# Turned input fetched piece by piece over the second down sweep, and a fourth raw buffer that lies in its last quarter

## The chip, the cores and the metric

One core of one Trainium2 chip. The metric is the device time in microseconds (us) of one launch, the median of three runs. The engines are named as the profile names them: PE (TensorE) for matmuls, PEld its weight loads, DVE (VectorE), ACT (ScalarE), POOL (GpSimd), SP (SyncE, which here only issues DMAs). A "q" behind a name (SPq, POOLq, ACTq) is that engine's instruction queue where it issues DMAs.

## The reference

Two layers over 256 tokens of width D = 2048 in float32. Layer 0 mixes tokens by a convolution module, layer 1 by latent attention; each is followed by the same kind of MLP, and a final RMSNorm ends the kernel. The change touches the MLP only:

```python
def sq_relu_mlp(h, w1, w2):                 # w1 (2048, 8192), w2 (8192, 2048)
    return jnp.square(jax.nn.relu(h @ w1)) @ w2
...
    for layer in range(DEPTH):
        ...
        h = rms_norm(x, norm_mlp_g[layer])
        x = x + sq_relu_mlp(h, mlp_w1[layer], mlp_w2[layer])
    return rms_norm(x, final_norm_g)
```

## The kernel before

**Products in three terms.** Every float32 operand is split into an upper part `hi` (ACT copies it to a narrower format, L460) and a lower part `lo` (DVE subtracts, L461), and a product is three matmuls, `mm3` (L213 to L215): hi by hi, lo by hi, hi by lo. Weights are split as they arrive; a "raw" buffer of 1 MB takes the load from HBM, and rings of `hi` and `lo` tiles (`WB` = 6) take its halves.

**The turned input.** The MLP's input is held transposed, in both parts: 16 blocks k of 128 features, each 2 KB in a partition, 32 KB in all (`xt`). It lies at the right end of the on-chip memory in two pools, one inside the other: level 0 holds blocks 0 to 3, level 1 holds blocks 4 to 7 in one tile and 8 to 15 in another. `open_xt` and `open_rest` open them, `xrows` finds a block.

**Two halves, and in each an up stage and two down sweeps.** `mlp` goes over the 8192 hidden features in two halves. A half first runs the up stage: 8 groups of 4 units, each unit one load of 4 blocks of `w1` (unit u of a group needs blocks 4u to 4u + 3 of the turned input) and 32 matmuls (L806, L807). Then come two down sweeps, one for each half of the output columns, of 16 units each: 7 plain ones (`PlainQuad`, 24 matmuls) and 9 mixed ones (`MixedQuad`, 21 matmuls on sums of weight blocks and of inputs, a scheme with seven products for eight). The order in the second sweep, numbered 0 to 15 here, is P M M P M P M M P M P M M P M P. The first units of the next half's up stage are called 16, 17, ... below. This structure stands twice, once in each layer; in each layer only the first half is followed by another half.

**Queues written out by hand.** `run` goes through the units. At each it first issues the loads for which a buffer is free, on SP. Then it queues the splits: the second half of the unit itself, the first half of the next unit, then (for a mixed unit) the sums of weight blocks on DVE (L511, L515, L516) and the splits of those sums; then the unit's matmuls, and then what is in `u.after`. The entries of `free` are the free buffers; those in `held` are not used again. Engines run their own queues in order, and a queue stands while its first instruction waits.

**A fourth raw buffer in the down sweeps.** Three raw buffers (`raw`) serve all stages. During the sweeps the level 1 pool of the turned input is closed, and `open_down` (called after the last up unit) opens another in its place: `forms` (8 KB, the last group's split inputs, which the plain units 0 and 3 of the second sweep are the last to read), `rawd`, a fourth raw buffer (8 KB), four `rooms` (8 KB, from which POOL adds the first sweep's sums to `xs` by DMA, L600) and a small pad.

**Saving and fetching.** In the first half the blocks 4 to 15 are saved to HBM during the up stage (`save`, L882, 6 DMAs of 512 KB). In the second sweep `retire_raw` takes `rawd` out of use after unit 7, and after unit 11 the level 1 pool is opened again and the blocks are fetched (`fetch`, L885) on SP: 4 and 6 after unit 11, 8 and 10 after unit 12, 12 and 14 after unit 13. In the profile these are `xt<-spare`. In the second half nothing is saved; at its end the pools are opened again for layer 1's mixer, or `load_gf` puts the final gain `gf` at level 0 (L2089, L2090), which DVE multiplies in (L2094) towards the end.

Beside the weights, the up stage of each half loads the corners that the mixed units need: `copy_sum` (SP, L874) and `add_sum` (POOL, L877), HBM to HBM.

Of the kernel before, what the change touches and what calls it, by code (L numbers as in the profile page):

```python
# [11 lines left out]
F32 = mybir.dt.float32  # L12
F32R = mybir.dt.float32r
# [6 lines left out]
P = 128  # L20
D = 2048
KC = D // P
T = 2
S = T * P
FF = 4 * D
NB = 512
# [54 lines left out]
def trunk_kernel(  # L81
# [60 lines left out]
    def nm(s):  # L142
        uid[0] += 1
        return f"{s}_{uid[0]}"
# [171 lines left out]
    at, cols = 0, []  # L316
# [8 lines left out]
    xt_cx, xt = [ExitStack(), ExitStack()], []  # L325
# [27 lines left out]
    def right_pool(name, bufs, level=0):  # L353

        for i in (1, 0)[: 2 - level]:
            xt_cx[i].close()
            xt_cx[i] = ExitStack()
        return xt_cx[level].enter_context(tc.tile_pool(name=name, bufs=bufs, side="right", reuse_waits="tile"))

    ctx.callback(lambda: [xt_cx[i].close() for i in (1, 0)])  # L360

    def xt_tile(pool, n):
        return pool.tile([P, n, 2 * S], F32R, name=nm("xt"))

    def open_xt(name):
        xt[:] = [xt_tile(right_pool(name, 1), KC // 4)]
        open_rest(name + "r")

    def open_rest(name):
        pool = right_pool(name, 1, 1)  # L370
        xt[1:] = [xt_tile(pool, n) for n in (KC // 4, KC // 2)]

    def xrows(k, n):
        i = min(k // 4, 2)
        return xt[i][:, k - 4 * i : k - 4 * i + n, :]

    xhl = lambda k: xrows(k, 1)[:, 0, :]
    xh = lambda k: xhl(k)[:, :S]
    xl = lambda k: xhl(k)[:, S:]
    open_xt("xt0")  # L380
    scratch = main.tile([P, NB], F32, name="scratch")

# [306 lines left out]
    def mlp(layer, ssq, next_gain, finish=None, before=None, between=None, beside=None, after_up=None):  # L689

        with ExitStack() as cx:
# [19 lines left out]
            units, rstd = [], []  # L711
# [6 lines left out]
            def open_down(hf):  # L718
                pool = right_pool(f"dn{layer}{hf}", 1, 1)
                down["forms"] = [pool.tile([P, 4, S], F32R, name=nm(f"d{c}")) for c in "hl"]  # L720
                raw = pool.tile([P, 4 * NB], F32, name=nm("rawd"))
                down["rooms"] = [pool.tile([P, NB], F32, name=nm("room")) for _ in range(4)]
                pool.tile([P, PAD_DOWN], F32, name=nm("pad"))
                down["raw"] = lambda: raw
                free.append(down["raw"])
# [134 lines left out]
            def half(hf):  # L860

                last = hf == HALVES - 1
# [18 lines left out]
                def save(k):  # L881
                    nc.sync.dma_start(spare[:, k : k + 2, :], xrows(k, 2).bitcast(F32))  # L882

                def fetch(k):
                    nc.sync.dma_start(xrows(k, 2).bitcast(F32), spare[:, k : k + 2, :])  # L885
# [6 lines left out]
                for g in range(ng):  # L892
# [13 lines left out]
                    for u in range(KC // 4):  # L906
                        n = KC // 4 * g + u

                        def multiply(q, g=g, u=u, ps=ps):
                            if u == 0:  # L910
                                ps[:] = [psum_bank(4 * (g % 2) + b) for b in range(4)]
                            up_products(ps, u, q.parts)

                        after = [lambda k=k: copy_sum(k) for k in due_at.get(n, [])]
                        after += [lambda k=k: add_sum(k) for k in due_at.get(n - 1, [])]
                        if not last and u == 2 and 1 <= g <= 6:
                            after.append(lambda g=g: save(2 * g + 2))
                        if u == KC // 4 - 1:
                            after.append(lambda g=g, ps=ps: at_ticks(evacuation(g, gs, ps)))
                            if beside is not None and hf == 0 and g == 1:  # L920
                                tables = beside()
                                after.append(lambda: at_ticks([(11 + 2 * i, lambda: next(tables, None)) for i in range(7)]))
                        if n == n_slots - 1:
                            after.insert(0, lambda: open_down(hf))
                        unit(Step, rows(mlp_w1[layer], 4 * u, 4, c0, NB), multiply, (), after)
# [5 lines left out]
                def mixed_unit(sums, i):  # L931
                    g, b = ms[i]

                    def src():
                        top, low = row_of((sums.n, i))
                        return top[:, :NB], low, made[sums.n, i]

                    unit(MixedQuad, src, lambda q: sums.mixed(q, *gs[g][b], i == len(ms) - 1))

                def plain_unit(sums, k, at=(), end=False):  # L940
                    unit(
                        PlainQuad, rows(w, k_lo + k, 2, sums.n * NB, 2 * NB),
                        lambda q: sums.plain(q.parts, hi, lo, k, end), at,
                    )

                for n in range(0, NNB, 2):
                    sums = Sums(n, (0, 1) if n == 0 else () if last else (1,))
                    final = last and n == NNB - 2
                    order = ks if n == 0 else ks[-2:] + ks[:-2]
                    head = HEAD[n // 2]  # L950
                    tail = LAST_TAIL if final and finish is not None else 2 if final else 1
                    inner = len(order) - head - tail
                    m, start = 0, len(units)
                    for i, k in enumerate(order[: len(order) - tail]):
                        plain_unit(sums, k)
                        if i < head - 1:
                            continue
                        upto = -(-len(ms) * (i - head + 2) // (inner + 1))
                        while m < upto:
                            mixed_unit(sums, m)  # L960
                            m += 1
                    if final:
                        for i in range(2):
                            units[-4 + i].after.append(lambda i=i: prepare(i, what="s"))
                        break
                    plain_unit(sums, order[-1], [lambda sums=sums: sums.join(room)], True)
                    closing.append([lambda sums=sums, n=n: sums.close(down_room if n == 0 else room)])
                    if n:
                        units[start + 7].after.append(retire_raw)
                        units[start + 11].after.append(lambda: open_rest(f"xt{layer}{hf}"))  # L970
                        for i, k in enumerate(range(KC // 4, KC, 2)):
                            units[start + 11 + i // 2].after.append(lambda k=k: fetch(k))
                if not last:
                    return

# [12 lines left out]
                def middle():  # L988
                    for n in range(2):
                        prepare(n, what="t")  # L990

                open_rest(f"xt{layer}{hf}")
                for k in tail:
                    end = k == tail[-1]
# [9 lines left out]
            for hf in range(HALVES):  # L1004
                nssq = half(hf)
# [4 lines left out]
    with ExitStack() as cx:  # L1010
# [235 lines left out]
        with tc.manual_schedule():  # L1246
# [100 lines left out]
            upper_x, lower_x, last = ((0, 0),), ((0, 1),), ((1, 0),)  # L1347
# [48 lines left out]
            for c in range(1, KC + 1):  # L1396
                n = UC * c
# [121 lines left out]
            for m in range(NP):  # L1519
# [4 lines left out]
                for j in range(2):  # L1524
                    k = 2 * m + j
# [19 lines left out]
                for q in {NP - 3: (0, 1, 4), NP - 2: (5, 2, 3), NP - 1: (6, 7)}.get(m, ()):  # L1545
                    t, i = divmod(q, NNB)
# [80 lines left out]
    with ExitStack() as cx:  # L1627
        at = cx.enter_context(tc.tile_pool(name="at", bufs=1, reuse_waits="tile"))
# [22 lines left out]
        units, pieces = [], {}  # L1651
# [297 lines left out]
        with tc.manual_schedule():  # L1949
# [89 lines left out]
            for g in range(NG):  # L2039
                for i in range(HG):  # L2040
                    h = g * HG + i

                    n = -(-len(work) // (HG - i))
# [29 lines left out]
            prefetch()  # L2073

        open_xt("xt1")
        ssq, add, prepare = residual_stage(
            True, g_mlp[1], raw=cq.rearrange("p t n -> p (t n)").rearrange("p (k s) -> p k s", s=S), by_steps=(2, 3)
# [103 lines left out]
```

## Time and profile before

| | us |
|---|---|
| median of 3 runs | 1945.93 |
| lowest, highest | 1945.91, 1948.66 |
| profiled execution | 1943.44 |
| its span | 1941.7 |
| PE busy in the span | 1922.1 |
| DVE busy | 1541.8 |
| ACT busy | 1150.3 |
| POOL busy | 315.0 |

The profile is of one execution, and its times are from the span's start. Its lines give, in a timeline: start, duration, engine, line of the kernel, operation, what it writes and reads, shapes, how many such were merged, and in brackets the idle time before it with what ended it. In a list of waits: engine, tile and line, who was waited for, total us, times, longest. In a table of windows: the stretch, its length, busy time and count of PE, PEld, DVE, ACT and POOL, the granted TensorE clock as a share of full speed, the mean busy share of the 16 DMA engines, and GB/s.

### The profile page before, as it was taken

Reading aid. Unit: us, or ns where it says so; the run is one execution under the profiler, and the core shown is the slowest. Engines: PE = TensorE matmul, PEld = TensorE weight load, DVE = VectorE, ACT = ScalarE, POOL = GpSimd, SP = SyncE. Lnnn points to the kernel's source line nnn. Section 1 sums busy time; section 2 is a strip of 40 time slices with the busy share of each in tenths; the row PEclk is TensorE's granted clock in tenths of the full one; section 3 lists DMA queues with packets and bytes.
Section 4 is the critical chain, followed back from the end, with each engine's and each line's share of the span. In section 5 each row is a group of like instructions: output and inputs, shape, how many; then the busy total and the mean of one; then the engine's idle time right before and its main releaser. Section 6 shows DMA issues by size and latency. Waiting matters only on the chain.

```text
span 1941.7 us, 29140 instructions
## 1 busy us (share of the span) xinstructions
PE 1922.1 (99%) x10775; PEld 1678.7 (86%) x10775; DVE 1541.8 (79%) x2472; ACT 1150.3 (59%) x1736; POOL 315.0 (16%) x284
## 2 busy tenths in 40 slices
PE   8999999999999999999999999999999999999998
PEld 8999888888888888888899998888888878888886
DVE  7999987767988676698976665866689976668998
ACT  5667755565665555666676665555556655555665
POOL 6999200110010100001001310001000101000010
PEclk9999999999999999999999999999999999999999
DMA  7766456997687988668665445499866889886683
GB/s 230 212 188 183 158 189 208 280 287 233 225 242 232 289 257 250 191 222 234 211 193 155 130 143 184 163 267 290 261 203 212 241 283 277 245 252 222 197 257 131
DMA packets 252590, 428.50 MB, mean 221 GB/s; under 512 B 21144, under 2 KB 96160, under 8 KB 252192
## 3 DMA queue, kind: packets, MB, share of 16 engines
q1 hardware_dynamic: 234992, 394.75, 62.1%
q0 software_dynamic: 16128, 29.37, 9.3%
q10 hardware_dynamic: 1328, 2.52, 0.4%
q8 instruction: 84, 1.38, 0.3%
q14 instruction: 58, 0.48, 0.1%
HBM read 407.72 MB, written 46.14 MB: 234 GB/s over the span
## 4 chain that ended last, share of the span: by engine, by line
PE 92%; DVE 3%; issue 2%; ACT 1%; DMA 0%; POOL 0%; ACTq 0%; DVEq 0%; POOLq 0%
PE acc L806 24%; PE acc L213 14%; PE acc L215 14%; PE acc L214 14%; PE acc L807 13%; PE acc L1075 8%; PE acc L1538 2%; DVE sum L1162 1%; ACT hi L180 0%; DMA xs<-in_x 0%; PE acc L1928 0%; DVE lo L184 0%; PE tr L277 0%; PE tr L1919 0%; PE acc L1792 0%
## 5 line engine op out<-in xcount | busy, mean ns | idle before, releaser
L461 DVE TENSOR_TENSOR lo<-raw,hi 128x1024 fp32r<-128x1024 f32 (+1 forms) x550 | 626.7, 1164 | 259.2 <-ACT hi L460 257.2
L460 ACT ACTIVATE hi<-raw 128x1024 fp32r<-128x1024 f32 (+1 forms) x550 | 541.6, 1010 | 298.7 <-DMA raw<-in_mlp_w 100.1
L806 PE MATMUL acc<-xt,hi 128*128 128x512 f32 x2048 | 710.5, 390 | 0.0
L807 PE MATMUL acc<-xt,lo 128*128 128x256 f32 x2048 | 577.5, 282 | 0.0
L806 PEld LDWEIGHTS acc<-xt,hi 128*128 128x128 f32 x2048 | 384.3, 188 | 80.5
L807 PEld LDWEIGHTS acc<-xt,lo 128*128 128x128 f32 x2048 | 387.3, 189 | 0.2
L180 ACT ACTIVATE hi<-raw 128x1024 fp32r<-128x1024 f32 (+2 forms) x210 | 206.3, 1008 | 62.8 <-PE acc L214 44.9
L184 DVE TENSOR_TENSOR lo<-raw,hi 128x1024 fp32r<-128x1024 f32 (+2 forms) x145 | 165.3, 1160 | 63.0 <-ACT hi L180 59.2
L215 PE MATMUL acc<-lo,sh 128*128 128x512 f32 x512 | 200.3, 391 | 0.8 <-DVE lo L461 0.8
L213 PE MATMUL acc<-hi,sh 128*128 128x512 f32 x512 | 201.0, 393 | 0.0
L877 POOL DMA_DIRECT2D q<-in_mlp_w x72 | 59.9, 832 | 771.8 <-DMA q<-in_mlp_w 755.8
L1075 PE MATMUL acc<-xt,hi 128*128 128x256 f32 x1024 | 180.1, 281 | 0.3 <-ACT b L1357 0.2
L214 PE MATMUL acc<-hi,sl 128*128 128x512 f32 x448 | 175.8, 392 | 0.0
L1162 DVE SCALAR_TENSOR_TENSOR sum<-ub,w_dw,sum 128x256 f32<-128x256 f32 x409 | 164.3, 482 | 3.5 <-ACT sum L1132 3.0
L184 POOL TENSOR_TENSOR lo<-raw,hi 128x1024 fp32r<-128x1024 f32 x65 | 155.1, 2410 | 17.3 <-ACT hi L180 17.3
L1075 PEld LDWEIGHTS acc<-xt,hi 128*128 128x128 f32 x1024 | 154.6, 188 | 1.1 <-ACT xt L1341 0.6
L1075 PE MATMUL acc<-xt,lo 128*128 128x256 f32 x512 | 139.2, 279 | 0.0
L818 ACT ACTIVATE v<-acc 128x256 f32<-128x256 f32 x128 | 45.2, 383 | 135.3 <-PE acc L807 135.2
L215 PEld LDWEIGHTS acc<-lo,sh 128*128 128x128 f32 x512 | 96.1, 188 | 24.0 <-DVE lo L461 2.8
L213 PEld LDWEIGHTS acc<-hi,sh 128*128 128x128 f32 x512 | 96.2, 188 | 20.8
L600 POOL DMA_DIRECT2D xs<-v x24 | 21.1, 944 | 553.4 <-ACT v L608 374.8
L460 ACT ACTIVATE hi<-rawd 128x1024 fp32r<-128x1024 f32 (+1 forms) x80 | 78.5, 981 | 54.5 <-PE acc L214 23.4
(331 smaller groups left out, 3178.3 us busy)
## 6 DMA issues: line engine op xcount, KB each, us to landing
raw<-in_mlp_w SPq DMA_DIRECT2D x172, 1024.0 KB, 7.4
raw<-in_conv_w_pw SPq DMA_DIRECT2D x62, 512.0 KB, 5.1
raw<-in_mlp_w SPq DMA_DIRECT2D x58, 512.0 KB, 5.4
q<-in_mlp_w SPq DMA_DIRECT2D x72, 256.0 KB, 8.2
q<-in_mlp_w POOLq DMA_DIRECT2D x72, 256.0 KB, 6.6
raw<-in_conv_w_pw SPq DMA_DIRECT2D x16, 1024.0 KB, 5.0
raw<-in_mla_w_o SPq DMA_DIRECT2D x16, 1024.0 KB, 5.4
raw<-q SPq DMA_DIRECT2D x58, 256.0 KB, 5.9
```

The source lines that it names most:

```text
L180: nc.scalar.activation(hi, raw[:, js, :], AF.Copy)
L184: eng.tensor_tensor(lo, raw, hi.bitcast(F32), op=ALU.subtract)
L213: nc.tensor.matmul(ps, sh, mh, start=start, stop=False)
L214: nc.tensor.matmul(ps, sl, mh, start=False, stop=False)
L215: nc.tensor.matmul(ps, sh, ml, start=False, stop=stop)
L460: nc.scalar.activation(hi, src, AF.Copy)
L461: nc.vector.tensor_tensor(lo, src, hi.bitcast(F32), op=ALU.subtract)
L806: nc.tensor.matmul(ps[b], wh[:, bs], xhl(k), start=k == 0, stop=False)
L807: nc.tensor.matmul(ps[b][:, :S], wl[:, bs], xh(k), start=False, stop=k == KC - 1)
L877: nc.gpsimd.dma_start(made[key], row_of(key)[0][:, :NB], accum_op=ALU.add)
L1075: nc.tensor.matmul(pss[c][b][:, :S], w[i][:, bs], (xh, xl)[j](k), start=k == i + j == 0, stop=end and k == k0 + nk - 1 and (i, j) == terms ...
L1162: nc.vector.scalar_tensor_tensor(out=out, in0=ubs[c][:, w : w + S], scalar=tap(c, w), in1=base, op0=ALU.mult, op1=ALU.add)
```

## The change

- The level 0 pool now has two tiles, blocks 0 to 3 ("first") and blocks 12 to 15 ("last"). Level 1 holds blocks 4 to 11 in one tile ("rest").
- `rawd` is no longer a tile of the pool that `open_down` opens. It is the "last" tile of level 0, opened with another type (`open_last`); forms, rooms and pad stay in the level 1 pool.
- `retire_raw` moves from after unit 7 to after unit 11.
- The level 1 pool is opened again after unit 4 instead of 11, and the blocks 4, 6, 8 and 10 are fetched after units 5, 7, 9 and 11, one DMA each.
- After unit 15 `open_last` opens blocks 12 to 15, and 12 and 14 are fetched there.
- At the end of the last half "last" is opened again before the rest.

```diff
-    def xt_tile(pool, n):
-        return pool.tile([P, n, 2 * S], F32R, name=nm("xt"))
+    def xt_tile(pool, n, tag):
+        return pool.tile([P, n, 2 * S], F32R, tag=tag, name=nm("xt"), bufs=1)
 
     def open_xt(name):
-        xt[:] = [xt_tile(right_pool(name, 1), KC // 4)]
+        pool = right_pool(name, 1)
+        xt[:] = [xt_tile(pool, KC // 4, "first"), pool, None, None]
+        open_last()
         open_rest(name + "r")
 
+    def open_last(kind=F32R):
+        xt[3] = xt[1].tile([P, KC // 4, 2 * S], kind, tag="last", name=nm("xt"), bufs=1)
+        return xt[3]
+
     def open_rest(name):
-        pool = right_pool(name, 1, 1)
-        xt[1:] = [xt_tile(pool, n) for n in (KC // 4, KC // 2)]
+        xt[2] = xt_tile(right_pool(name, 1, 1), KC // 2, "rest")
 
     def xrows(k, n):
-        i = min(k // 4, 2)
-        return xt[i][:, k - 4 * i : k - 4 * i + n, :]
+        i, at = ((0, 0), (2, 4), (2, 4), (3, 12))[k // 4]
+        return xt[i][:, k - at : k - at + n, :]
...
-                raw = pool.tile([P, 4 * NB], F32, name=nm("rawd"))
+                raw = open_last(F32).rearrange("p k n -> p (k n)")
...
                     if n:
-                        units[start + 7].after.append(retire_raw)
-                        units[start + 11].after.append(lambda: open_rest(f"xt{layer}{hf}"))
-                        for i, k in enumerate(range(KC // 4, KC, 2)):
-                            units[start + 11 + i // 2].after.append(lambda k=k: fetch(k))
+                        units[start + 4].after.append(lambda: open_rest(f"xt{layer}{hf}"))
+                        for i, k in enumerate(range(KC // 4, 3 * KC // 4, 2)):
+                            units[start + 5 + 2 * i].after.append(lambda k=k: fetch(k))
+                        units[start + 11].after.append(retire_raw)
+                        units[start + 15].after.append(open_last)
+                        for k in (12, 14):
+                            units[start + 15].after.append(lambda k=k: fetch(k))
...
+                open_last()
                 open_rest(f"xt{layer}{hf}")
```

## The prediction

> **What bounds the kernel now.** I read the page first, then who PE waited for, then PE's own timeline where those waits lie.
>
> ```profile
> span 1941.7 us, 29140 instructions
> PE 1922.1 (99%) x10775; PEld 1678.7 (86%) x10775; DVE 1541.8 (79%) x2472; ACT 1150.3 (59%) x1736; POOL 315.0 (16%) x284
> ...
> PE acc L215 <- DVE lo L461: 4.2, 4, 1.4
> ```
>
> TensorE has work 99% of the span, so a change that alters no matmul can win only where PE stands. The last row is the largest wait that PE has inside the kernel's loops: the third matmul of a triple needs a lower half `lo` that VectorE has not written. Three of its four waits, and all the longer ones, lie in unit 14 of the second sweep, two in layer 0's first half and one in layer 1's. PE's timeline there, first layer 0, then layer 1:
>
> ```profile
> 626.16 0.39 PE L213 MATMUL acc<-hi,gh 128*128 128x512 f32 x1
> ...
> 631.65 0.39 PE L213 MATMUL acc<-hi,mh 128*128 128x512 f32 x1
> ...
> 634.62 0.40 PE L214 MATMUL acc<-hi,ml 128*128 128x512 f32 x1
> 636.46 0.50 PE L215 MATMUL acc<-lo,mh 128*128 128x512 f32 x1 [1.44 <-DVE lo L461]
> ...
> 638.73 0.51 PE L215 MATMUL acc<-lo,mh 128*128 128x512 f32 x1 [0.99 <-DVE lo L461]
> ...
> 639.77 0.39 PE L213 MATMUL acc<-hi,gh 128*128 128x512 f32 x1
> ...
> 1579.38 0.39 PE L213 MATMUL acc<-hi,mh 128*128 128x512 f32 x1
> ...
> 1586.06 0.39 PE L213 MATMUL acc<-hi,gh 128*128 128x512 f32 x1
> ...
> 1591.55 0.40 PE L806 MATMUL acc<-xt,hi 128*128 128x512 f32 x1
> ```
>
> Unit 13 is plain: 24 matmuls in 631.65 - 626.16 = 5.49 us, 0.229 us each. Unit 14 is mixed, 21 matmuls, so 4.81 us. It took 639.77 - 631.65 = 8.12 us in layer 0 and 1586.06 - 1579.38 = 6.68 us in layer 1. The loss is 3.31 and 1.87 us, together **5.18 us**. That is all there is to gain at this place. What made `lo` late is in the timelines of ScalarE and VectorE:
>
> ```profile
> 632.28 2.53 ACT L460 ACTIVATE hi<-raw 128x1024 fp32r<-128x1024 f32 x3 [7.09 <-DMA raw<-in_mlp_w]
> 633.37 1.23 DVE L461 TENSOR_TENSOR lo<-raw,hi 128x1024 fp32r<-128x1024 f32 x1 [6.04 <-ACT hi L460]
> ...
> 635.72 2.95 DVE L461 TENSOR_TENSOR lo<-raw,hi 128x512 fp32r<-128x512 f32 x3
> ...
> 1578.56 2.53 ACT L460 ACTIVATE hi<-raw 128x1024 fp32r<-128x1024 f32 x3 [5.12 <-DMA raw<-in_mlp_w]
> ```
>
> ScalarE stood 7.09 us for a weight load, that of unit 15. `run()` queues unit 15's first split ahead of unit 14's last ones, so the late load holds up unit 14. Why it was late is in the queue of SyncE (SP). The two rows of landings are those of the loads issued at 623.23 and 1583.85.
>
> ```profile
> 581.38 0.38 SPq L476 DMA_DIRECT2D raw<-in_mlp_w  x1
> ...
> 618.26 0.80 SPq L885 DMA_DIRECT2D xt<-spare  x2
> 623.23 0.38 SPq L476 DMA_DIRECT2D raw<-in_mlp_w  x1
> 623.65 0.94 SPq L885 DMA_DIRECT2D xt<-spare  x2
> ...
> DMA to landing us min/median/max: 8.9/8.9/8.9
> ...
> 1570.96 0.38 SPq L476 DMA_DIRECT2D raw<-in_mlp_w  x1
> 1583.85 0.38 SPq L476 DMA_DIRECT2D raw<-in_mlp_w  x1
> ...
> DMA to landing us min/median/max: 5.4/5.4/5.4
> ```
>
> Unit 15's load (623.23; 1570.96 in layer 1) has a pair of fetches just ahead of it and another just behind: 2 MB beside its own. It took 8.9 us. The load of 1583.85, the same 1 MB with another load 1.1 us behind it but no fetch, took 5.4 us. The DMA share by stretch, from the windows view (last two columns):
>
> ```profile
> 618.00:634.00 16.00, 16.00 (x72) 13.13 (x71) 9.73 (x11) 7.61 (x9) 0.00 (x0) 1.00 0.94 308
> ...
> 636.00:638.00 2.00, 1.23 (x3) 0.48 (x3) 2.00 (x3) 2.00 (x3) 0.00 (x0) 1.00 0.04 15
> 1582.00:1584.00 2.00, 1.95 (x7) 0.76 (x5) 2.00 (x4) 1.83 (x3) 0.00 (x0) 1.00 0.15 56
> 1586.00:1634.00 48.00, 48.00 (x270) 42.15 (x270) 31.25 (x44) 21.44 (x29) 7.67 (x9) 1.00 1.03 311
> ```
>
> The engines are full (0.94, 308 GB/s) while the fetches run, empty for a moment while PE stands, and full again (1.03) for the first 48 us of the second half's up stage.
>
> **The change, part by part.** No compute instruction is added or removed; the same 12 fetches of 512 KB move.
>
> *Unit 15's load.* With `rawd` kept to unit 11 there are four buffers until then. Unit 11 goes into `rawd`, units 12 to 14 load one buffer earlier, and unit 15 is issued when unit 13's second split is done, as now. So the issue stays at 623.23 and 1570.96, but the nearest fetch (10) is issued behind unit 14's load, about two units (10 us) earlier, and none stands behind. Taking 5.4 us, it lands at 628.6 and 1576.4. What it must meet: unit 14's last `lo` ended at 635.72 + 2.95 = 638.67, which is 6.5 us after the landing at 632.1, and PE wants it before the unit's 18th matmul, 17 x 0.229 = 3.89 us after its start, at 635.54. So landing by 629.0 is early enough, and by the same reckoning 1576.8 in layer 1 (6.39 us from ScalarE's 1578.56 to the last `lo`). Margin 0.4 us in each. I take the whole 5.18 us as gone. Bounds: 0 (it still lands as late as now) and 5.18. Late next, if anything, is the same `lo`.
>
> In the Trainium skill, page "DMA: Bandwidth & Descriptors", section "Bandwidth", 1 MB is listed at 6.15 us (issued from GpSimd). By it unit 15 would land 0.3 to 0.4 us too late in each layer, and the time would be some 0.7 us above mine, an estimate. The row of 5.4 us from this kernel's own queue is nearer, and I go by it.
>
> *Four fetches moved forward (after units 5, 7, 9, 11).* Each costs SP 0.4 to 0.5 us of issue and moves 512 KB. The first waits for the forms (last matmul in unit 3) and the rooms; behind it on SP stands unit 9's load. The last room's transfer and its landing:
>
> ```profile
> 570.95 0.86 POOL L600 DMA_DIRECT2D xs<-room  x1 [0.20 <-issue]
> ...
> DMA to landing us min/median/max: 7.7/7.7/7.7
> ```
>
> It is down at 578.6. The fetch follows unit 8's load of 581.38. Units 4 to 12, six mixed and three plain ones, lie between unit 3's last matmul and unit 13's start, so that matmul ends at 626.16 - 6 x 4.81 - 3 x 5.49 = 580.8. So nothing waits: cost 0, covered by loads that run several us ahead of their splits. If that cover were gone, each us of landing would fall on unit 9.
>
> *The pair after unit 15 (k = 12 and 14).* Its wait on `rawd` is long over: unit 11's splits end four units earlier. On SP it stands between the loads of units 17 and 18, 0.9 us of issue, and adds 1.05 MB at 311 GB/s = 3.4 us to a DMA system that is then full. PE needs it at unit 19, over 20 us later. Who pays is the loads behind, units 18 to 23. What slack they have now, from VectorE's splits and PE's start of the up units:
>
> ```profile
> 661.05 2.36 DVE L461 TENSOR_TENSOR lo<-raw,hi 128x1024 fp32r<-128x1024 f32 x2 [5.40 <-ACT hi L460]
> ...
> 1597.12 0.39 PE L806 MATMUL acc<-xt,hi 128*128 128x512 f32 x1
> ...
> 1608.24 2.36 DVE L461 TENSOR_TENSOR lo<-raw,hi 128x1024 fp32r<-128x1024 f32 x2 [4.96 <-ACT hi L460]
> ...
> 1625.41 1.23 DVE L461 TENSOR_TENSOR lo<-raw,hi 128x1024 fp32r<-128x1024 f32 x1 [1.68 <-ACT hi L460]
> ```
>
> An up unit is 1597.12 - 1591.55 = 5.56 us. Layer 1: unit 20's first half is split at 1608.24 + 1.2 = 1609.4 and wanted at 1591.55 + 4 x 5.56 = 1613.8, slack 4.4; unit 23's at 1626.6 against 1630.5, slack 3.8. Layer 0: up starts at 639.77 + 5.49 = 645.26, unit 20's at 662.3 against 667.5, slack 5.2. Without the stall PE wants everything 1.87 (3.31) us sooner. But unit 17's load, which now waits for unit 15's split, also goes out sooner by what unit 15 lands earlier: 2.2 us in layer 1 (1578.56 to 1576.4), 3.5 in layer 0 (632.1 to 628.6). So the work behind is later by 3.4 - 2.2 = 1.2 us and -0.1 us, and the slack left is 3.8 - 1.87 - 1.2 = 0.7 us and 5.2 - 3.31 + 0.1 = 2.0 us. No stall: 0. Bounds: -0 (it cannot help) to 1.5 us in each layer if the earlier start is worth nothing (3.8 - 1.87 - 3.4 = -1.5; 5.2 - 3.31 - 3.4 = -1.5).
>
> *The last quarter in one pool with the first.* At the end of layer 1 `gf` is allocated at that level. Now it lies on the first quarter and its load goes out as soon as the last group's first unit is done. If it comes to lie on the last quarter, it must wait for `rawd`'s last split:
>
> ```profile
> 1752.64 0.33 ACTq L2090 DMA_DIRECT2D gf<-in_final_norm_g  x1
> ...
> 1900.06 0.68 DVE L2094 TENSOR_TENSOR xs<-xs,gf 128x512 f32<-128x512 f32 x1
> ...
> 1907.29 1.89 DVE L461 TENSOR_TENSOR lo<-rawd,hi 128x512 fp32r<-128x512 f32 x2
> ...
> 1925.00:1930.00 5.00, 5.00 (x24) 4.09 (x23) 4.61 (x11) 1.75 (x5) 0.00 (x0) 1.00 0.00 0
> 1930.00:1935.00 5.00, 3.79 (x29) 3.43 (x27) 4.49 (x14) 2.55 (x7) 0.00 (x0) 1.00 0.58 210
> ```
>
> So at 1909.2 instead of 1752.64, landing 5.4 us later at 1914.6, while two gains (L2094) stand at 1900 to 1902 today. Moved behind 1914.6 they are 2 x 0.6 = 1.2 us of VectorE, which idles 0.39 + 0.51 = 0.9 us between 1925 and 1935 where the kernel's end is made. Bounds 0 (the place is the first quarter) and 14.5 us (VectorE stands from 1900.06 for the landing). I take 0.3 us, the 1.2 that does not fit into 0.9. The diff does not say which quarter it is.
>
> *Elsewhere* (the openings before layer 1's mixer and in `open_xt`): the tiles under them are read last by matmuls that PE has passed before the new writes; 0.
>
> Sum, on the profiled execution: its own time is 1943.44 us (span 1941.7 and 1.7 around it); -5.18 + 0 + 0 + 0.3 = -4.9, so 1938.5. That execution is 2.5 us below the median of the three runs, 1945.93; the same saving off the median gives **1941.1 us**.
>
> **The rivals.**
> 1. *The stall shrinks only.* Unit 15's issue does not move, only its company. The median landing of such loads is 7.4 us by the page's list of DMA issues:
>
> ```profile
> raw<-in_mlp_w SPq DMA_DIRECT2D x172, 1024.0 KB, 7.4
> ```
>
> At 7.4 it lands 1.6 us past the limit in layer 0 (3.31 becomes 1.6) and as late as now in layer 1. Gain 1.7 to 2: 1944. For it: the margin is 0.4 us. Against: 7.4 is a median over full DMA stretches.
> 2. *The wait moves into the up stage.* The pair delays units 20 to 23 by its whole 3.4 us: 1.5 us lost in each layer, gain 2.2: 1943.8. For it: the share of 1.03. Against: the empty stretches of 0.04 and 0.15, which the pair can fill.
> 3. *The change doesn't reach further than noise*: the stall of an ordinary run is another one; 1945.9.
> 4. *Slower: `gf`.* It lies on `rawd`, and VectorE's or ScalarE's queue waits for it in order. Each us past what PE has in hand goes to the end; it cancels the gain at 5.2 us and is slower by over 0.2% from 9.1 us on. With the full 14.5 us the time is 1945.93 - 5.18 + 14.5 = 1955. For it: VectorE is full until 1925. Against: what is not ready need not be queued at 1900.
>
> **How the numbers follow.** 0.2% is 3.9 us, about what a measurement here can tell from no change. The forecast holds 0.50, with its own range 1938.0 to 1942.0: at the low end the 2.5 us by which ordinary runs exceed the profiled one are also stalls of this kind (1943.44 - 5.18 = 1938.3), at the high end `gf` costs the 1.2 us. Rival 1 has 0.18, rival 2 0.10, rival 3 0.05, `gf` 0.17, of which 0.09 for a price of 1.3 to 9 us and 0.08 above. Faster: the forecast, 0.50. Within 0.2%: 0.18 + 0.10 + 0.05 + 0.09 = 0.42. Slower: 0.08. The range 1938.0 to 1946.0 takes in all but the slower end of `gf` and a little of either side.
>
> **What would show it.** Right: unit 14 takes 4.8 us in both layers; unit 15's load lands in 5 to 6 us; ScalarE's wait for it falls from 7.09 and 5.12 us to under 4; fetches stand singly after units 5, 7, 9 and 11, a pair behind unit 17's load; PE has no wait in the first 50 us of the second halves. Wrong: a PE wait on `lo` at units 18 to 23; an SP wait before the first fetch past 581; `gf` issued near 1900 with a hole on VectorE, or PE waiting in the last 40 us.

## The result, and the profile after

| | before | after |
|---|---|---|
| median | 1945.93 us, 9 runs | 1941.62 us, 9 runs |
| lowest, highest | 1944.23, 1949.23 | 1941.04, 1941.88 |
| profiled execution, its span | 1943.44, 1941.7 | 1941.04, 1939.3 |

The ratio is 0.9974, 95% interval 0.9963 to 0.9984. The forecast was 1941.1 us. (One of the nine executions of the changed kernel, 3208.51 us at a granted clock of 0.556, was disturbed and is left out of the highest and of the ratio.) Lines have moved: the splits are now L465 (ACT) and L466 (DVE), the plain loads L481, the fetches L890, the gains L2103. The fourth raw buffer, `rawd` before, now appears as `xt`.

The page's first lines and PE's largest wait in the loops:

```profile
span 1939.3 us, 29128 instructions
PE 1920.7 (99%) x10775; PEld 1678.4 (87%) x10775; DVE 1541.1 (79%) x2472; ACT 1149.5 (59%) x1736; POOL 315.8 (16%) x284
...
PE acc L215 <- DVE lo L466: 1.7, 3, 0.8
```

The wait for `lo` has gone from 4.2 us in four waits to 1.7 in three. Two of the three are what is left in unit 14. PE's timeline, layer 0 and then layer 1; the first and the last row of each group are the starts of units 14 and 15:

```profile
631.90 0.39 PE L213 MATMUL acc<-hi,mh 128*128 128x512 f32 x1
...
635.56 0.40 PE L214 MATMUL acc<-hi,ml 128*128 128x512 f32 x1
636.36 0.50 PE L215 MATMUL acc<-lo,mh 128*128 128x512 f32 x1 [0.40 <-DVE lo L466]
636.70 0.40 PE L213 MATMUL acc<-hi,mh 128*128 128x512 f32 x1
...
637.39 0.39 PE L213 MATMUL acc<-hi,gh 128*128 128x512 f32 x1
...
1576.56 0.39 PE L213 MATMUL acc<-hi,mh 128*128 128x512 f32 x1
...
1581.05 0.51 PE L215 MATMUL acc<-lo,mh 128*128 128x512 f32 x1 [0.43 <-DVE lo L466]
...
1582.10 0.39 PE L213 MATMUL acc<-hi,gh 128*128 128x512 f32 x1
```

Unit 14 takes 637.39 - 631.90 = 5.49 us in layer 0 (8.12 before) and 5.54 in layer 1 (6.68 before), where 4.81 would be free of waits. So 2.63 + 1.14 = **3.77 us** were won there and 0.68 + 0.73 = **1.41 us** are still lost. SP's queue, the landing of the load that it issued at 623.47 (unit 15's), and ScalarE's and VectorE's answer to it:

```profile
610.33 0.52 SPq L890 DMA_DIRECT2D xt<-spare  x1
623.47 12.09 SPq L481 DMA_DIRECT2D raw<-in_mlp_w  x3
635.61 0.97 SPq L890 DMA_DIRECT2D xt<-spare  x2
...
DMA to landing us min/median/max: 6.3/6.3/6.3
...
629.91 2.53 ACT L465 ACTIVATE hi<-raw 128x1024 fp32r<-128x1024 f32 x3 [4.48 <-DMA raw<-in_mlp_w]
633.35 2.95 DVE L466 TENSOR_TENSOR lo<-raw,hi 128x512 fp32r<-128x512 f32 x3
...
618.00:623.00 5.00, 5.00 (x24) 4.10 (x23) 4.80 (x6) 3.88 (x5) 0.00 (x0) 1.00 0.00 0
```

The last fetch ahead stands at 610.33, the pair at 635.61, and the DMA engines are empty for 5 us before the load goes out (the window's DMA share, 0.00; 0.88 before). Still the load took 6.3 us. It was not alone: the row of 623.47 holds three loads, and the second of them, unit 16's, goes out 1.1 us behind it, at 624.61. The last row of unit 14's splits ends at 633.35 + 2.95 = 636.30, and the matmul at 636.36 had waited for it.

At the kernel's end there is a new loss. The gain's load and the last split that reads the fourth raw buffer:

```profile
1903.21 1.90 DVE L466 TENSOR_TENSOR lo<-xt,hi 128x512 fp32r<-128x512 f32 x2
1905.14 0.33 ACTq L2099 DMA_DIRECT2D gf<-in_final_norm_g  x1
...
1918.10 3.49 DVE L184 TENSOR_TENSOR lo<-raw,hi 128x1024 fp32r<-128x1024 f32 x3
1921.51 2.49 DVE L2103 TENSOR_TENSOR xs<-xs,gf 128x512 f32<-128x512 f32 x4
1923.92 1.88 DVE L403 TENSOR_TENSOR xs<-acc,xs 128x512 f32<-128x512 f32 x3
```

`gf` is issued at 1905.14, just as that split ends (1903.21 + 1.90), instead of at 1752.64. Four gains stand in a row after the last splits. Of before, the same stretch:

```profile
1922.20 3.49 DVE L184 TENSOR_TENSOR lo<-raw,hi 128x1024 fp32r<-128x1024 f32 x3
1925.61 0.68 DVE L2094 TENSOR_TENSOR xs<-xs,gf 128x512 f32<-128x512 f32 x1
1926.43 1.38 DVE L398 TENSOR_TENSOR xs<-acc,xs 128x512 f32<-128x512 f32 x2
```

There only one gain stands at this place; three of the others had been done earlier, from 1900.06 on. From the start of these last three splits to the end of the span it is 1941.7 - 1922.20 = 19.5 us before and 1939.3 - 1918.10 = 21.2 after: **1.7 us** lost. Up to that point the changed kernel was 1922.20 - 1918.10 = 4.1 us ahead: 3.77 in unit 14 and 0.3 in other places (above all two waits in layer 1's mixer that fell from 1.1 to 0.5 us together; every other trace here has the 1.1, so this looks like chance). 4.1 - 1.7 = 2.4 is the whole difference of the two spans.

### The profile page after: what moved, and what is told of

Same layout as the page of the kernel before. It is cut to its first block, busy times and chain, and to the rows that moved or that the text cites. A ratio compares the mean times of both kernels' runs of the same rounds, so it can differ in the third digit from the quotient of the medians.

```text
span 1939.3 us, 29128 instructions
## 1 busy us (share of the span) xinstructions
PE 1920.7 (99%) x10775; PEld 1678.4 (87%) x10775; DVE 1541.1 (79%) x2472; ACT 1149.5 (59%) x1736; POOL 315.8 (16%) x284
## 4 chain that ended last, share of the span: by engine, by line
PE 96%; DVE 3%; ACT 0%; DMA 0%; issue 0%; ACTq 0%; DVEq 0%
PE acc L811 24%; PE acc L213 15%; PE acc L215 15%; PE acc L214 15%; PE acc L812 13%; PE acc L1084 8%; PE acc L1547 2%; DVE sum L1171 1%; DMA xs<-in_x 0%; PE acc L1826 0%; PE acc L1825 0%; PE acc L1824 0%; PE tr L277 0%; PE acc L1801 0%; PE acc L1802 0%; PE acc L1803 0%
## 5 line engine op out<-in xcount | busy, mean ns | idle before, releaser
L466 DVE TENSOR_TENSOR lo<-raw,hi 128x1024 fp32r<-128x1024 f32 (+1 forms) x542 | 618.3, 1165 | 255.7 <-ACT hi L465 251.9
L465 ACT ACTIVATE hi<-raw 128x1024 fp32r<-128x1024 f32 (+1 forms) x542 | 533.8, 1010 | 291.6 <-DMA raw<-in_mlp_w 96.7
L465 ACT ACTIVATE hi<-xt 128x1024 fp32r<-128x1024 f32 (+1 forms) x88 | 86.2, 979 | 61.0 <-PE acc L214 24.1
```

Of the source, the lines that this page charges most:

```text
L465: nc.scalar.activation(hi, src, AF.Copy)
L466: nc.vector.tensor_tensor(lo, src, hi.bitcast(F32), op=ALU.subtract)
```

## The experiments

All are variants of the changed kernel but the last two, which are variants of the kernel before. Every median stands beside runs of the kernel before on the same chip: 1946.1 us for the first four, 1945.82 for the next four, 1945.68 for the last two. In each of the three groups the runs of before are spread over some 6 us, so the ratios have wide intervals; the variants' own spreads are 0.8 to 2.4 us, but for `before_pair15` with 4. The changed kernel's own 1941.62 us is of another occasion, on which the kernel before had 1945.93, so a few tenths of a us between a variant and it say little.

**1. Is it the placement of the buffers or the place of the fetches?** `old_schedule` keeps the new memory plan with the old order:

```diff
-units[start + 4].after.append(lambda: open_rest(...))
-for i, k in enumerate(range(KC // 4, 3 * KC // 4, 2)):
-    units[start + 5 + 2 * i].after.append(lambda k=k: fetch(k))
-units[start + 11].after.append(retire_raw)
-units[start + 15].after.append(open_last)
-for k in (12, 14): units[start + 15].after.append(...)
+units[start + 7].after.append(retire_raw)
+units[start + 11].after += [open_last, lambda: open_rest(...)]
+for i, k in enumerate(range(KC // 4, KC, 2)):
+    units[start + 11 + i // 2].after.append(lambda k=k: fetch(k))
```

> The changed kernel's memory plan with the old order: the fourth raw buffer retired after unit 7, all blocks fetched in pairs after units 11, 12 and 13. Theory A: unit 14 is back at 6.7 to 8.1 us, unit 15's load takes 7.5 to 9 us, and with gf's 1.5 us on top the median is 1945.9 + 1.5 = 1947.4. Theory D (the gain came from where the tiles lie, not from when they are fetched): 1941.6.

Measured: 1948.77 us (1947.49 to 1949.84), ratio 1.0014, interval 1.0005 to 1.0023. The wait is back:

```profile
PE acc L215 <- DVE lo L466: 5.1, 5, 1.3
```

The new memory plan alone makes the kernel 0.14% slower; the gain is the order's. (The median is 1.4 us above the expectation. The trace is of the fastest execution, 1947.49 us; in it some 1.4 us were lost in layer 1 beside the waits, where TensorE's clock was halved, see the last section. That such losses lift the median is likely but not shown: the traced execution has a mean granted clock of 0.998, nine of the other ten 0.997.)

**2. Does the longer stay of the fourth buffer matter?** `retire7`:

```diff
-units[start + 11].after.append(retire_raw)
+units[start + 7].after.append(retire_raw)
```

> The changed kernel with the fourth raw buffer retired after unit 7 again; the fetches stay spread. Theory A (what counts is that no fetch stands beside unit 15's load): unit 14 takes 5.5 us and the median is the changed kernel's, 1941.6, within 0.5. Theory B (what counts is the buffer that stays longer, so that units 11 to 14 load earlier): the stall comes back, 1944 to 1946.

Measured: 1941.58 us (1941.19 to 1942.89), ratio 0.9977, interval 0.9968 to 0.9986: the same as the changed kernel. The stay from unit 7 to 11 brings nothing.

**3. What would the up stage have charged for more fetches there?** `pair_twice` fetches blocks 8 and 10 a second time behind unit 15:

```diff
-for k in (12, 14):
+for k in (12, 14, 8, 10):
     units[start + 15].after.append(lambda k=k: fetch(k))
```

> The changed kernel with blocks 8 and 10 fetched once more after unit 15, behind 12 and 14: 1 MB of the same data on top at the place where the prediction feared the loads of units 18 to 23. By the prediction's arithmetic (3.1 to 3.4 us later, each us beyond the slack lost; the changed kernel's least slack is 2.5 us, layer 1, unit 20): 0.6 to 0.9 us lost in layer 1 and 0 to 0.5 in layer 0, so 1942.2 to 1943.0. Rival (the transfers have room there after all): 1941.6. Rival (there is no slack, both layers pay in full): 1948.

Measured: 1943.8 us (1943.12 to 1943.94), ratio 0.9987, interval 0.9978 to 0.9996. Waits in the up stage appear that no other kernel here has:

```profile
PE acc L812 <- DVE lo L466: 0.8, 3, 0.3
```

So 2 MB there cost 2.2 us more than 1 MB by medians, above the 0.6 to 1.4 expected. In the traces the up stage itself is longer by 0.6 us in layer 0 and 1.0 in layer 1. The three waits lie at units 18 and 19, ahead of the units 20 to 23 that the prediction feared for. The 1 MB of the change fits in.

**4. Late gains.** The first try, `gf_first`, opened the two tiles of the level 0 pool in the other order:

```diff
-xt[:] = [xt_tile(pool, KC // 4, "first"), pool, None, None]
-open_last()
+xt[:] = [None, pool, None, None]
+open_last()
+xt[0] = xt_tile(pool, KC // 4, "first")
```

> The changed kernel with the two tiles of level 0 opened in the other order, so that the final gain gf should come to lie on blocks 0 to 3 again and not on the fourth raw buffer. Theory A (the gain came from unit 15's load, and some 1.5 us of it were lost at the kernel's end because gf's load waits for the fourth raw buffer): gf is issued near 1748 us instead of 1905, two of DVE's multiplications by gf stand near 1896 again, unit 14 still takes 5.5 us, and the median is 1.5 us below the changed kernel's 1941.6, so 1940.1. Theory C (the loss at the end has another cause, such as four multiplications of DVE that end later for any reason): 1941.6, with the end as in the changed kernel.

Measured: 1941.87 us (1941.51 to 1942.91), ratio 0.9979, interval 0.9970 to 0.9987. The load did not move:

```profile
1905.27 0.33 ACTq L2100 DMA_DIRECT2D gf<-in_final_norm_g  x1
```

So the theory was not tested: whichever tile `gf` would lie on, it came out as late. The second try, `gf_in_first`, opens no new pool:

```diff
+def open_first(kind):
+    return xt[1].tile([P, KC // 4, 2 * S], kind, tag="first", name="gf", bufs=1)
...
-gfs.append(right_pool("gf", 1).tile([P, D], F32, name="gf"))
+gfs.append(open_first(F32).rearrange("p k n -> p (k n)")[:, :D])
```

> The changed kernel, but the final gain's tile takes the room of the first quarter of the turned input in the pool that is already open, instead of a new pool that opens only when the whole of the old one is free. Theory A (the new pool's first tenant waits for every tile of the old pool, the fourth raw buffer in it too, and the gains that follow late cost about 1.5 us at the end): the gain's load is issued near 1748 us instead of 1905, the first gains run near 1900 instead of 1921, the span falls to about 1937.8 us and the median to 1940.1 us (1939.7 to 1940.7). Rival A' (the end is long for another reason, the late gains being idle time of VectorE): the load moves, the median stays at 1941.6 us. Rival A'' (the load waits for something else than the pool): issue stays at 1905 us, median 1941.6 us.

Measured: 1940.37 us (1939.90 to 1941.38), ratio 0.9975, interval 0.9965 to 0.9986.

```profile
1749.00 0.33 ACTq L2102 DMA_DIRECT2D gf<-in_final_norm_g  x1
...
1918.61 3.49 DVE L184 TENSOR_TENSOR lo<-raw,hi 128x1024 fp32r<-128x1024 f32 x3
1922.01 0.68 DVE L2106 TENSOR_TENSOR xs<-xs,gf 128x512 f32<-128x512 f32 x1
1922.84 1.38 DVE L406 TENSOR_TENSOR xs<-acc,xs 128x512 f32<-128x512 f32 x2
```

The load is early again, one gain stands where four stood, and the tail is 1938.1 (the span) - 1918.61 = 19.5 us, as before the change. By medians it is 1.25 us faster than the changed kernel, by the tail 1.7. With `gf_first` this says: a new pool at this level waited for every tile of the old one, a tile of the old pool only for the tile that it follows.

**5. What is left in unit 14.** `keep15` lets the fourth buffer serve one load more, so that unit 15's load need not wait for one of the other three:

```diff
-units[start + 11].after.append(retire_raw)
-units[start + 15].after.append(open_last)
-for k in (12, 14): units[start + 15].after.append(...)
+units[start + 15].after.append(retire_raw)
+carry.append((start + 16, [open_last] + [lambda k=k: fetch(k) for k in (12, 14)]))
...
+for at, todo in carry:
+    units[at].after[:0] = todo
```

> The changed kernel, but the fourth raw buffer serves one load more (retired after unit 15 of the sweep instead of unit 11) and the last pair is fetched after the first up unit (16) instead of after unit 15. Theory C (what is left of the wait in unit 14, 0.68 us in layer 0 and 0.73 us in layer 1 of the changed kernel's trace, is unit 15's load, 6.3 us long and issued when the third buffer comes free): that load is issued about 4.8 us earlier, unit 14 takes 4.8 us in both layers, the median falls by 1.4 us to 1940.2 us (1939.8 to 1940.8). Rival (the pair, now 4.8 us later, is late in the up stage): waits on TensorE appear in the first six up units and eat 0.5 to 2 us, median 1941 to 1942.5 us. Rival (unit 14's remainder isn't the load): unit 14 stays at 5.5 us, median 1941.6 us.

Measured: 1940.23 us (1939.93 to 1941.64), ratio 0.9975, interval 0.9965 to 0.9985.

```profile
618.20 0.38 SPq L481 DMA_DIRECT2D xt<-in_mlp_w  x1
...
DMA to landing us min/median/max: 5.7/5.7/5.7
...
624.83 11.11 SPq L481 DMA_DIRECT2D raw<-in_mlp_w  x3
636.00 0.97 SPq L890 DMA_DIRECT2D xt<-spare  x2
...
PE acc L215 <- DVE lo L466: 0.8, 1, 0.8
```

The load stands at 618.20, into the fourth buffer (`xt`), and the row of landings is its own: with nothing issued within its flight it took 5.7 us. Unit 14 runs without a gap in both layers, 4.81 us; the 0.8 that is left is a wait at another place, which the kernel before had too. 1.4 us were expected and 1.39 came, which is closer than the spreads allow one to claim.

`halves` leaves the issue where it is and cuts each plain 1 MB load in two:

```diff
+def load(self, raw):
+    self.raw = raw.rearrange("p (j n) -> p j n", j=2)
+    for j in range(2):
+        nc.sync.dma_start(self.raw[:, j : j + 1, :], self.src[:, j : j + 1, :])
```

> The changed kernel, but each 1 MB load of a plain unit is issued as two transfers of 512 KB, so that the splits of the first half can start when it has landed. Theory C (the remainder in unit 14 is the length of unit 15's load): its first half lands near 627 us instead of 629.8, unit 14 takes 4.8 us, median 1940.2 us (1939.7 to 1941). Rival (the two halves run side by side on the same DMA engines and land together, or the added issues of SP cost as much as they bring): unit 14 stays near 5.5 us, median 1941.6 to 1942.5 us.

Measured: 1940.60 us (1940.39 to 1941.66), ratio 0.9973, interval 0.9963 to 0.9983. ScalarE's rows around the load:

```profile
627.77 1.58 ACT L465 ACTIVATE hi<-raw 128x1024 fp32r<-128x1024 f32 x2 [1.89 <-DVE lo L466]
629.87 1.06 ACT L465 ACTIVATE hi<-raw 128x1024 fp32r<-128x1024 f32 x1 [0.52 <-DMA raw<-in_mlp_w]
```

The first half is split from 627.77 on, the second lands no sooner than the whole did. Unit 14 takes 4.81 us in both layers. So the remainder was the wait for the whole megabyte, of which the first split needs half. (By medians 1.0 us came. In the trace unit 14 gives the whole 1.4, but 0.5 us of it are lost again at the kernel's very end; why stays open.)

**6. Both repairs.** `best` is `gf_in_first` and `keep15` together.

> Both of the two other edits together: the final gain in the room of the first quarter, and the fourth raw buffer kept through unit 15 with the last pair after unit 16. If theories A and C hold and the two add: 1941.6 - 1.5 - 1.4 = 1938.7 us (1938.2 to 1939.6), unit 14 at 4.8 us in both layers and the gain's load issued near 1748 us. If only one holds, 1940.2 us; if neither, 1941.6 us.

Measured: 1938.46 us (1938.41 to 1939.47, 5 runs), ratio 0.9966, interval 0.9954 to 0.9979; span 1936.5. The gains of the two parts, 1.25 and 1.39, add up to 2.64, and 3.16 came; the difference of 0.5 us is within the spreads. It is faster than both kernels.

**7. How little of the change is needed?** In the kernel before, `before_pair15` moves only the third pair:

```diff
-units[start + 11 + i // 2].after.append(lambda k=k: fetch(k))
+units[start + (11, 12, 15)[i // 2]].after.append(lambda k=k: fetch(k))
```

> The kernel before with its own memory plan, and only the third pair of fetches moved, from after unit 13 to after unit 15: the second pair still goes out just ahead of unit 15's load (618.3 us), nothing just behind it. Theory F (transfers share the engines, so those behind a load slow it as well as those ahead): unit 15's load lands near 630.8 us instead of 632.2, unit 14 loses about 2 us in layer 0 and 1.2 in layer 1 instead of 3.3 and 1.9, the gain's load stays near 1752 us, median 1944 us (1943 to 1945) where before is 1945.9. Rival (a queue serves in order, only what is ahead counts): the load still takes 8.9 us, median 1945.9 us. Rival (only what is behind counts): it lands at 629.5 to 629.8, median 1941 to 1942 us.

Measured: 1942.37 us (1941.24 to 1945.21), ratio 0.9984, interval 0.9975 to 0.9992. SP's queue, and the landing of the load of 623.49:

```profile
618.58 0.79 SPq L885 DMA_DIRECT2D xt<-spare  x2
623.49 13.79 SPq L476 DMA_DIRECT2D raw<-in_mlp_w  x3
...
DMA to landing us min/median/max: 8.0/8.0/8.0
```

8.0 us, against 8.9 with a pair on either side (8.6 in `old_schedule`) and 6.3 with none. It landed at 631.5 us, where theory F had 630.8 and the two rivals 632.2 and 629.5 to 629.8. Unit 14 loses 2.4 us in layer 0 and 0.9 in layer 1. So, by one trace of each kernel, the pair behind the load delays it, against the rival of strict order, and the pair ahead delays it more, against the other rival. The median is 1.6 us better than theory F said; the trace, at 2.4 + 0.9, is near its 2 + 1.2. With runs 4 us apart, the difference stays unexplained.

`before_11_11_15` also moves the second pair, to unit 11:

```diff
-units[start + 11 + i // 2].after.append(lambda k=k: fetch(k))
+units[start + (11, 11, 15)[i // 2]].after.append(lambda k=k: fetch(k))
```

> The kernel before with its own memory plan, the second pair fetched after unit 11 with the first, the third after unit 15, so that no fetch stands near unit 15's load. If only the place of the fetches counts (neither the spreading to single ones nor the fourth buffer's longer stay): unit 14 loses 0.7 us in each layer as in the changed kernel, the gain's load stays near 1752 us, so that the late gains' 1.5 us are not paid: 1941.6 - 1.5 = 1940.1 us (1939.6 to 1941). Rival (2 MB behind unit 11 crowd the loads of units 13 and 14 as 2 MB crowded unit 15's): waits on TensorE in units 12 to 14 take the place of the old one, 1942 to 1946 us.

Measured: 1940.45 us (1939.48 to 1940.93), ratio 0.9973, interval 0.9962 to 0.9983.

```profile
609.56 2.55 SPq L885 DMA_DIRECT2D xt<-spare  x4
...
623.78 12.27 SPq L476 DMA_DIRECT2D raw<-in_mlp_w  x3
...
DMA to landing us min/median/max: 6.5/6.5/6.5
...
636.84 0.50 PE L215 MATMUL acc<-lo,mh 128*128 128x512 f32 x1 [0.58 <-DVE lo L461]
```

Unit 15's load takes 6.5 us, unit 14 loses 0.87 and 0.62 us, and `gf` stays early. With one line of the old kernel, no new memory plan and no spreading, it is faster than the changed kernel, whose lowest run, 1941.04 us, lies above all 8 of this one (the two were measured on different occasions).

## Why the prediction was right, and where it was off

**The stall in unit 14: right.** `old_schedule` and `before_11_11_15` show from both sides that the fetches around unit 15's load made it late and that this was the stall.

**The chain behind the load: right to 0.1 us.** The prediction had 6.5 us from landing to the last `lo`; after, the load landed at 623.47 + 6.3 = 629.8, and 636.3 - 629.8 = 6.5. Its limit of 629.0, moved by the later start of the unit (631.90 instead of 631.65), is 629.25. The loss of 0.68 us is the 0.55 by which the landing missed it and a slow step behind the gap (636.36 to 636.70, 0.34 us instead of 0.23).

**Its duration: the step that failed.** The 5.4 us were those of another load, of an up unit. Unit 15's took 6.3, and so 1.41 us of the 5.18 stayed. The surroundings were alike: no fetch near, and the next load 1.1 us behind. What differed was the load itself, `w2` for a down unit instead of `w1` for an up unit, and that was not looked at. Why the one takes longer stays open. The next load counts too: alone, in `keep15`, unit 15's took 5.7 us. At that it would have landed at 629.2, just in time, so the margin of 0.4 us would have held by less than 0.1. In the Trainium skill, page "DMA: Bandwidth & Descriptors", section "Bandwidth", the 6.15 us for 1 MB were nearer (a figure for the transfer without its issue), and the estimate of 0.7 us left over, given beside it, was on the right side, at half the size. The signs that the prediction set itself say the same: unit 14 takes 5.5 us and not 4.8, the load 6.3 and not 5 to 6, and ScalarE's wait is 4.48 us and not under 4. For unit 14 rival 1 had the mechanism, a stall that only shrinks; its gain of 1.7 to 2 us was too small.

**Four fetches moved forward: 0, right.** No wait of TensorE on units 5 to 12 appeared, and the first stands at 582.26, when the forms and rooms are free.

**The pair behind unit 15: 0, right, and rival 2 falls.** In the windows of the up stages PE stays full with the DMA engines as full as before (1.04 and 1.02, second to last column; layer 1 had 1.03 before):

```profile
1586.00:1634.00 48.00, 48.00 (x276) 42.42 (x275) 27.96 (x39) 23.52 (x35) 6.73 (x8) 1.00 1.04 316
642.00:690.00 48.00, 48.00 (x277) 42.48 (x276) 27.90 (x40) 23.80 (x35) 6.72 (x8) 1.00 1.02 312
```

That the slack was nearly used up, as it said (0.7 us left in layer 1, 2.0 in layer 0), is not borne out: by its own 3.4 us for 1 MB, `pair_twice` would have lost 2.7 and 1.4 us there, and its trace lost 1.0 and 0.6.

**`gf`: the wait was right, the price wrong.** The prediction weighed whether `gf` would lie on the last quarter; in fact it follows the whole pool. It was issued at 1905.1 (1909.2 said), with no hole on VectorE, and three gains, not two, moved into the end. There they stand in a row ahead of the last work, so the 0.9 us of idle time behind them, which was counted on, took up none of them: 3 x 0.6 = 1.8 us. 1.7 us by the tail and 1.25 by medians stand against 0.3; that is the low end of rival 4's price (1.3 to 9 us), though no queue stood for `gf` as rival 4 had it.

**The sum.** On the profiled executions: -5.18 + 1.41 + 1.7 - 0.3 = -2.4, where the prediction had -4.9. By medians it was -4.3. The nearness of 1941.1 to 1941.62 is in part luck: two terms were too hopeful by 1.4 us each (the load's duration and `gf`), and the profiled execution of before lay 2.5 us under its median, a surplus that the prediction carried over to the changed kernel and of which only 0.6 us (1941.62 - 1941.04) were left there. That such a surplus is itself stall was in the prediction as the low end, 1943.44 - 5.18 = 1938.3; `best`, with neither the stall nor the late gains, has 1938.46. So the ordinary run of before loses some 7 us to this stall, not 5.18, an inference from the medians, since only one run of before has a trace. Why it varies from run to run stays open. The record has one lead. Of the 70 runs of before that stand beside the experiments, the 15 with a mean granted clock of 0.999 have a median of 1944.2 us, the 35 with 0.998 one of 1945.8 and the 20 with 0.997 one of 1947.5; the profiled one has 0.999. So the surplus goes with time at a lower TensorE clock, and `old_schedule` shows this stall lowering it. That it does so in those runs no trace shows.

## What to carry to other kernels

Take the duration of a transfer from a row of the same tensor, shape and surroundings, and let it decide whether a margin of 0.4 us holds. When a load is late, look at what is issued within its own flight on either side: moving the neighbours by a few units was worth all of the gain here, and the buffer plan built for it none. A pool that got a longer-lived tenant made `gf`, the first tile of its successor, wait for that tenant; look for the next user of the room.

## What the runs showed of the hardware

A short gap can halve TensorE's clock. In `old_schedule`, layer 1, unit 14 had two waits in 4 us, and then five matmuls in a row started 0.43 us apart instead of 0.23 (PE's timeline and the windows, granted clock in the third column from the right):

```profile
1583.73 0.50 PE L215 MATMUL acc<-lo,mh 128*128 128x512 f32 x1 [1.29 <-DVE lo L466]
...
1586.00 0.79 PE L215 MATMUL acc<-lo,mh 128*128 128x512 f32 x1 [0.99 <-DVE lo L466]
1586.59 0.63 PE L213 MATMUL acc<-hi,mh 128*128 128x512 f32 x1
1587.02 0.63 PE L214 MATMUL acc<-hi,ml 128*128 128x512 f32 x1
...
1582.00:1586.00 4.00, 1.67 (x5) 0.49 (x5) 4.00 (x6) 2.92 (x5) 0.00 (x0) 0.95 0.19 60
1586.00:1589.00 3.00, 3.00 (x7) 2.42 (x8) 2.96 (x6) 0.60 (x1) 0.12 (x1) 0.50 0.95 283
```

The granted clock is 0.50 for 3 us, and some 1.4 us are lost beside the waits. In the Trainium skill, page "TensorE: Matmul & The Clock Gate", section "Part 1: The HAM clock gate (the "warmup" mystery)", matmuls of 512 columns are given 426.7 ns from start to start at the halved clock, and this run agrees (0.43 us). The same page of the Trainium skill has the clock fall after at least one idle window of some 3.4 us; here no single wait was longer than 1.3 us. So a stall that is split into two waits close together can cost more than it shows. It need not: the kernel before had such a pair in layer 0 (1.44 and 0.99 us, 636.46 and 638.73), and `old_schedule` too (1.05 and 0.99), and the granted clock stayed at 1.00 behind both. What decides isn't shown.

Megabyte loads from the same queue took 5.4 us (an up unit's, before, the next load 1.1 us behind it), 5.7 (unit 15's in `keep15`, nothing issued within its flight), 6.3 (unit 15's, after, the next load 1.1 us behind it) and 8.0 to 8.9 (unit 15's with 1 or 2 MB of fetches near).
